# A lasting weight ring of five tiles instead of three, and one weight tile in the memory of the expert sum

## The chip, the core and the metric

The kernel runs on one core of a Trainium2 chip, as one launch. The metric is the time of that launch on the device in microseconds, the median of several runs. The engines of the core work through their own instruction streams and wait for each other by semaphores: TensorE (PE) multiplies matrices, VectorE (DVE), ScalarE (ACT) and GpSimd (POOL) work elementwise, SyncE (SP) does nothing but issue DMA transfers. ScalarE and GpSimd issue some transfers, too.

## The reference

The reference is a network of two layers on 256 tokens x and, beside them, 256 context tokens, all of width 1024. Cut to what matters:

```python
for l in range(2):
    mod = silu(c) @ w_ada[l] + b_ada[l]              # six vectors of 1024; the same for the context
    h = x * (1 + mod[1]) + mod[0]
    parts = split(h @ w_in[l])                       # 1024 -> 2592 columns
    y = concat(diff_attention(parts[0:3]), mla_attention(parts[3:6]), retention(parts[6:10])) @ w_out[l]
    x = layer_norm(ALPHA * x + mod[2] * y)
    h = x * (1 + mod[4]) + mod[3]
    tokens = concat(h, h_of_context)                 # the context in the first layer alone
    scores = sigmoid(tokens @ router_w)              # 16 experts in 4 groups; best group, best 2 in it
    f = sum over the two chosen experts e of gate[e] * (silu(tokens @ w1[e]) * (tokens @ w3[e])) @ w2[e]
    x = layer_norm(ALPHA * x + mod[5] * f)
```

All is float32. The weights are some 300 MB, and each is read once, or in the part that is needed.

## The kernel before, in words

The weights come as tiles of 128 x 2048 float32, 1.05 MB each. The class `Stream` (from line 124) owns them. A list written in advance (`want_ada`, `want_win`, `want_wout`, `want_exp`, up to line 333) sets the order in which they are used, and so the order in which SyncE loads them: the modulation weights `w_ada`, the input projection `w_in`, the output projection `w_out`, then the experts of the layer, and the same for the second layer. Tiles live in rings. A ring (`add_ring`, line 140) is a pool of so many buffers; `pump` (line 154) issues a load for the next tile of the list as long as a ring has a free buffer, and `done` gives a buffer back behind the last instruction that reads the tile. The next load into that buffer waits for that instruction. A newly made ring is filled at once. Besides rings there are rooms (`add_rooms`): memory that belongs to something else and holds one weight tile each until it is wanted.

The lasting ring has RA tiles and exists for the whole program. Per layer there are two more, of sizes RB: one that exists from the end of the attention, and one that is added when the routing is known. The second layer has a ring of four half tiles beside them. The first expert tiles of a layer can be loaded before the routing is known (a tile of the plan stands for one or two experts, and most are fixed in advance); `known` marks how many.

Float32 weights are mostly used in two parts: a rounded high part (`wh`, a cast on ScalarE or, for the first two output-projection tiles, on GpSimd at line 415) and the rest (`wl`, a subtraction on VectorE or GpSimd, line 416 or 1223), with three products for each on TensorE.

The order in which instructions stand on each engine is found by a scheduler, which plays the program through with estimated times, except in stretches where TensorE's order is written out by hand. A changed ring therefore also changes the order elsewhere. Each DMA that SyncE or ScalarE issues takes one of eight semaphores in turn, and can only be issued when the transfer that used it before has landed.

Lines that are spoken of: 187 and 183 (loads of whole tiles and of halves), 1160 (loads of the inputs `xs`), 658 (transposes of `xs`), 530 and 499 (modulation products), 430 to 432 (the three products of a projection), 905, 921 and 942 (transposes in the attention), 558 (transposes of `rt`, the modulation rows), 1644, 1741, 1616 (expert products), 1679 (stores of finished expert rows `yd`), 574 (loads of layer-norm rows), 1962 (gathers `fr` of expert rows), 221 (the helper that records all of ScalarE's and VectorE's work).

Of the kernel before, what the change touches and what calls it, by code (L numbers as in the profile page):

```python
# [23 lines left out]
LAM_INIT = [0.8 - 0.6 * math.exp(-0.3 * l) for l in range(DEPTH)]  # L24
NE = 16
BIG = 8192.0

CHUNKS = [("q", 384), ("k", 384), ("v", 384), ("m", 416), ("qg", 512), ("kv", 512)]
CHUNK_COLS = {
# [196 lines left out]
def build(tc, x_in, ctx_in, wada, win, wout, wexp, wqkv, rw, prm_in, bro_in, lnr, cst_in, out, dbg=None):  # L226
    nc = tc.nc
# [3 lines left out]
    G, T, S = nc.gpsimd, nc.tensor, nc.sync  # L231
# [104 lines left out]
    ws = Stream(nc, aps, widths)  # L336
# [5 lines left out]
    hlp = es.enter_context(tc.tile_pool(name="hlp", bufs=4))  # L342
    ps = es.enter_context(tc.tile_pool(name="ps", bufs=2, space=PS))
    dr = es.enter_context(tc.tile_pool(name="dr", bufs=1, space=DRAM))
    RA, RB = 3, ((4, 3), (3, 6))

    cst = cp.tile([128, NCST], F32, name="cst")
    prm = cp.tile([128, NPRM], F32, name="prm")
# [48 lines left out]
    def level():  # L397
        load["A"] = load["V"] = 0.0
# [10 lines left out]
    def split(raw, n, pool=None, tags=("wh", "wl"), sub=None, high=None, into=None):  # L409

        h, lo = into() if into else ((pool or hlp).tile([128, 1024], F32R, tag=t, name=t) for t in tags)
        if high is None:
            A.copy(h[:, :n], raw)
        else:
            high.tensor_copy(h[:, :n], raw)
        (sub or V).tensor_tensor(lo[:, :n], raw, h[:, :n].bitcast(F32), op=ALU.subtract)
        return h[:, :n], lo[:, :n]
# [717 lines left out]
    x1t = {}  # L1135
# [45 lines left out]
    for l in range(DEPTH):  # L1181
        last = l == DEPTH - 1
# [14 lines left out]
        def wout_half(pool, tags):  # L1197
            for half in range(2):
                raw = ws.take()
                for q in range(2):  # L1200
                    pieces.append(split(raw[:, 1024 * q:1024 * q + 1024], 1024, pool, tags, V if pool else G, high=None if pool else G))
                ws.done()

        wout_half(None, ("wh", "wl"))
        by_time = (0, 1, 2, 6, 7, 3, 4, 5)
        for b in by_time:
# [60 lines left out]
        for i in tiles:  # L1267
# [8 lines left out]
            for n in range(2):  # L1276
                o = acc() if n else sbig()[:, 0:512]
                os_.append(o)
                for k in by_time:
                    h, lo = pieces[4 * n + k // 2]  # L1280
                    c = (k % 2) * 512
# [204 lines left out]
        def tiles_beyond():  # L1486

            nxf = small("nxf", [1])
            V.reduce_sum(nxf, VX.rearrange("p m e -> p (m e)"), axis=AX.X)
            nxi = small("nxi", [1], I32)  # L1490
            V.tensor_copy(nxi, nxf)
            return nc.values_load(nxi[0:1, 0:1], min_val=0, max_val=16 * NM,
                                  skip_runtime_bounds_check_because="at most so many tiles for each expert")
# [82 lines left out]
        def ones_at(t):  # L1576

            Os[t] = []
            for i in tiles:
                O = rp_.tile([128, 128], F32, tag="O", name="O", bufs=2 * NT)  # L1580
                for n, s in enumerate(slots_of(l, t)):
                    pos = (pos0 if s < 2 else posm)[:, i, s:s + 1]
                    if n == 0:
                        V.tensor_scalar(O, C("iota"), pos, None, op0=ALU.is_equal)
                    else:
                        V.scalar_tensor_tensor(O, C("iota"), pos, O, op0=ALU.is_equal, op1=ALU.add)
                Os[t].append(O)
# [67 lines left out]
        def hidden(t):  # L1655
            u = us[t]
            tp = tpb()
            for k in range(4):
                T.transpose(tp[:, 128 * k:128 * k + 128], u[:, 128 * k:128 * k + 128], ident)
            uH = ex.tile([128, 4, 128], F32R, tag="uH", name="uH", bufs=2)  # L1660
            d = uH.rearrange("p k t -> p (k t)")
            if len(plan[t]) == 1:
                uL = ex.tile([128, 4, 128], F32R, tag="uL", name="uL", bufs=2)
                A.copy(d, tp)
                V.tensor_sub(uL.rearrange("p k t -> p (k t)"), tp, d.bitcast(F32))
                us[t] = uH, uL
            else:
                copy(d.bitcast(F32), tp)
                us[t] = uH[:].bitcast(F32)
# [104 lines left out]
        if last:  # L1774

            at_slots()
            f = x1t["f"]
            G.memset(f, 0.0)
            gains1 = ex.tile([16, 128], F32, name="gains1")
            for n in range(2):  # L1780
                nc.scalar.dma_start(gains1[8 * n:8 * n + 8], lnr[n, l].rearrange("(k c) -> k c", c=128))
# [19 lines left out]
            def dispatch(j):  # L1801
                xs_of[j] = ex.tile([128, 8, 128], F32, tag="x", name="x", bufs=2)
                pick(xs_of[j], Os[j])

            def to_tokens(j):

                O = Os.pop(j)
                OTs[j] = rp_.tile([128, W], F32R, tag="OT", name="OT", bufs=3)
                transposed_ones(OTs[j], O)
                gms[j] = rp_.tile([128, 1], F32, tag="gp", name="gp", bufs=2)  # L1810
                gates_at(j, O, acc())(gms[j])
# [17 lines left out]
            with tc.manual_schedule(engines=only_pe):  # L1829
                up(0, [[], [lambda: to_tokens(0)], [], []])  # L1830
                ones_at(1)
                dispatch(1)
                hidden(0)
                down(0)
            level()
            beyond = tiles_beyond()
            m5r = ex.tile([128, 1024], F32, name="m5r")
# [85 lines left out]
        else:  # L1923
# [17 lines left out]
            def rows_of_tokens():  # L1941
                V.tensor_scalar(off_, posm, 127.5, BIG, op0=ALU.is_gt, op1=ALU.mult)
                V.tensor_scalar(place_, posm, 0.0, BIG, op0=ALU.is_lt, op1=ALU.mult)
                V.tensor_tensor(off_, off_, place_, op=ALU.add)
                V.tensor_tensor(place_, posm, C("row0")[:, None, :].to_broadcast([128, NT, 16]), op=ALU.add)
                V.tensor_tensor(place_, place_, off_, op=ALU.add)
                V.tensor_reduce(two[:, :, 0], place_, axis=AX.X, op=ALU.min)
                V.tensor_tensor(off_, place_, two[:, :, 0:1].to_broadcast([128, NT, 16]), op=ALU.is_equal)
                V.scalar_tensor_tensor(place_, off_, BIG, place_, op0=ALU.mult, op1=ALU.add)
                V.tensor_reduce(two[:, :, 1], place_, axis=AX.X, op=ALU.min)  # L1950
                V.tensor_scalar_min(two, two, float(ZROW))
                V.tensor_copy(twoi, two)
# [13 lines left out]
            def gather(x, ll):  # L1966

                gi = rp_.tile([128, 1], I32, tag="gi", name="gi", bufs=4)
                V.tensor_scalar(tmpi, ll[:, 1:2], 0.0, BIG, op0=ALU.is_equal, op1=ALU.mult)
                V.scalar_tensor_tensor(gi, ll[:, 1:2], -1.0, tmpi, op0=ALU.add, op1=ALU.add)  # L1970
# [305 lines left out]
```

## Time and profile before

| | us |
|---|---|
| median of 3 runs (lowest to highest) | 1275.64 (1275.26 to 1279.91) |
| profiled execution | 1273.33 |
| its span | 1271.6 |
| TensorE busy in it | 1142.1 (90%) |
| VectorE, ScalarE, GpSimd busy | 658.9, 472.1, 353.7 |
| mean granted TensorE clock | 0.945 of full |

The profile shows one execution. Its span runs from the first to the last instruction; what lies around it is launch and end. A granted clock of 1.00 means 2.4 GHz, 0.50 means 1.2 GHz. In a timeline each row is a run of equal instructions of one engine: start, length, engine, line, operation, what it writes and reads, how many; in brackets the idle time in front of it, and what ended that.

### The profile page before, as it was taken

The numbers are of one execution on the slowest core, as the hardware profiler recorded it, in microseconds if no ns is written. First come the engines' busy times: TensorE is split into PE (matmuls) and PEld (weight loads), VectorE is DVE, ScalarE is ACT, GpSimd is POOL, SyncE is SP. The second block draws the span as 40 slices with busy tenths as digits, with TensorE's granted clock in tenths as the row PEclk, the third lists the DMA queues.
The fourth block names the chain that finished last, engine by engine and source line by source line (L and its number), as shares of the span: only waits on it lengthen the run. The fifth ranks groups of instructions, "written<-read, shape, count | busy, mean of one in ns | idle before, by whom it ended". The sixth has DMA issues, their size and how long they took to land. (4 is left out here: it accounts for less than half of the span.)

```text
span 1271.6 us, 17886 instructions
## 1 busy us (share of the span) xinstructions
PE 1142.1 (90%) x6443; PEld 747.1 (59%) x6443; DVE 658.9 (52%) x1308; ACT 472.1 (37%) x870; POOL 353.7 (28%) x344
## 2 busy tenths in 40 slices
PE   5999999998996898998992889999998699999994
PEld 3898764566785755545351668976556644444431
DVE  3645366636478966546371768437536712222116
ACT  4423456335235554324241355446343210111102
POOL 0332220231044555335154457221221100101002
PEclk8999999998996898999996979999998799999997
DMA  9443008661546799999985212420764899999981
GB/s 365 160 140 130 1 1 322 262 248 65 208 158 237 248 397 413 409 392 414 414 363 132 76 51 79 153 77 16 283 265 169 317 410 408 409 409 408 409 331 58
DMA packets 72301, 311.77 MB, mean 245 GB/s; under 512 B 8576, under 2 KB 9232, under 8 KB 57872
## 3 DMA queue, kind: packets, MB, share of 16 engines
q1 hardware_dynamic: 63376, 287.73, 58.3%
q10 hardware_dynamic: 5952, 14.45, 3.1%
q0 software_dynamic: 2880, 8.39, 2.4%
q8 instruction: 53, 0.87, 0.3%
q14 instruction: 40, 0.33, 0.1%
HBM read 304.70 MB, written 7.93 MB: 246 GB/s over the span
## 5 line engine op out<-in xcount | busy, mean ns | idle before, releaser
L221 DVE TENSOR_TENSOR wl<-w,wh 128x640 fp32r<-128x640 f32 (+3 forms) x134 | 167.9, 1279 | 48.6 <-ACT wh L221 47.5
L221 ACT CAST wh<-w 128x1024 fp32r<-128x1024 f32 (+2 forms) x136 | 132.5, 1004 | 117.6 <-issue 39.8
L1223 POOL TENSOR_TENSOR wl<-w,wh 128x384 fp32r<-128x384 f32 x96 | 132.9, 1411 | 138.8 <-ACT wh L221 121.3
L1644 PE MATMUL s<-w,x 128*64 128x512 f32 (+1 forms) x640 | 115.8, 596 | 0.0
L221 DVE TENSOR_REDUCE mxv<-s 128x2 f32<-128x1024 f32 (+1 forms) x54 | 56.3, 1044 | 48.0 <-PE s L1098 20.1
L221 ACT ACTIVATE P<-s,mxv 128x512 f32<-128x512 f32 (+1 forms) x108 | 65.9, 618 | 41.1 <-DVE mxv L221 22.3
L1741 PE MATMUL s<-w,uH 128*32 128x512 f32 (+1 forms) x480 | 78.5, 595 | 0.0
L1644 PEld LDWEIGHTS s<-w,x 128*64 128x64 f32 (+1 forms) x640 | 33.6, 126 | 64.9 <-issue 61.2
L221 ACT ACTIVATE u<-s 128x512 f32<-128x512 f32 x20 | 11.9, 596 | 130.7 <-PE s L1644 111.2
L1644 PE MATMUL s<-w,xH 128*32 128x512 f32 (+1 forms) x384 | 56.6, 594 | 0.0
L430 PE MATMUL acc<-wh,hH 128*128 128x384 f32 (+3 forms) x148 | 53.1, 361 | 3.7 <-ACT hH L221 3.7
L431 PE MATMUL s<-wl,hH 128*128 128x384 f32 (+2 forms) x148 | 52.9, 357 | 2.9 <-DVE wl L221 2.9
L221 DVE SCALAR_TENSOR_TENSOR u<-u,gp,s 128x512 f32<-128x512 f32 x20 | 14.9, 744 | 77.6 <-ACT u L221 77.6
L221 DVE TENSOR_TENSOR yL<-s,yH 128x512 fp32r<-128x512 f32 x20 | 13.8, 688 | 76.6 <-ACT yH L221 76.5
L430 PE MATMUL s<-wh,hH 128*128 128x384 f32 (+2 forms) x148 | 53.0, 358 | 0.0
L432 PE MATMUL s<-wh,hL 128*128 128x384 f32 (+2 forms) x148 | 52.8, 357 | 0.0
L431 PE MATMUL acc<-wl,hH 128*128 128x384 f32 (+3 forms) x148 | 52.0, 351 | 0.6 <-DVE wl L221 0.6
L432 PE MATMUL acc<-wh,hL 128*128 128x384 f32 (+3 forms) x148 | 50.5, 351 | 0.0
L1741 PEld LDWEIGHTS s<-w,uH 128*32 128x32 f32 (+1 forms) x480 | 23.2, 122 | 45.0 <-issue 41.7
L1616 PE MATMUL s<-wh,xH 128*128 128x512 f32 x128 | 44.1, 428 | 5.4 <-ACT wh L221 5.4
L1616 PE MATMUL s<-wl,xH 128*128 128x512 f32 x128 | 44.3, 422 | 4.1 <-POOL wl L1223 2.1
L1788 POOL TENSOR_TENSOR xr<-xr,lr 128x1024 f32<-128x1024 f32 x4 | 9.4, 2358 | 135.0 <-ACT lr L221 135.0
(527 smaller groups left out, 2509.5 us busy)
## 6 DMA issues: line engine op xcount, KB each, us to landing
w<-in_wexp_dram SPq DMA_DIRECT2D x288, 512.0 KB, 10.1
w<-in_wexp_dram SPq DMA_DIRECT2D x48, 1024.0 KB, 10.4
w<-in_wada_dram SPq DMA_DIRECT2D x45, 1024.0 KB, 6.2
w<-in_win_dram SPq DMA_DIRECT2D x8, 1024.0 KB, 4.7
w<-in_wout_dram SPq DMA_DIRECT2D x8, 1024.0 KB, 6.7
w<-in_win_dram SPq DMA_DIRECT2D x9, 768.0 KB, 4.1
row<-rowd ACTq DMA_DIRECT2D x9, 512.0 KB, 12.6
yd<-rows ACTq DMA_DIRECT2D x18, 256.0 KB, 8.8
```

The source lines that it names most:

```text
L221: return f(*args, **kw)
L430: T.matmul(o, lhsT=lh, rhs=rh, start=start, stop=False, skip_group_check=True)
L431: T.matmul(o, lhsT=lh, rhs=rl, start=False, stop=False, skip_group_check=True)
L432: T.matmul(o, lhsT=ll, rhs=rh, start=False, stop=stop, skip_group_check=True)
L1223: G.tensor_tensor(lo[:, c:], raw[:, c:], h[:, c:].bitcast(F32), op=ALU.subtract)
L1616: T.matmul(o, lhsT=ll if ps_ == 2 else lh, rhs=rl if ps_ == 1 else rh, start=start and j == 0 and not (same and n), stop=stop and j == 2 a ...
L1644: T.matmul(o[r0:r1, halves[c // 2]], lhsT=x[:, kk, r0:r1], rhs=raw[e][:, halves[q]], start=(kk == 0), stop=(kk == 7), skip_group_check=True)
L1741: T.matmul(o[r0:r1, halves[n]], lhsT=u[:, kk, r0:r1], rhs=raw[e][:, halves[n]], start=(kk == 0), stop=(kk == 3), skip_group_check=True)
L1788: G.tensor_tensor(x1[:, i, :], x1[:, i, :], lr, op=op)
```

## The change

The lasting ring gets five tiles instead of three (RA). The two rings of each layer that come later get one tile less each (RB). In the second layer the memory of the expert sum, `f`, becomes a room for one weight tile behind the attention; so the clearing of `f` moves behind the first expert tile. The scratch in which GpSimd's DMAs keep their descriptors shrinks to 2 KB, which makes the room for the larger ring.

```diff
+SCRATCH = 2048
...
-    RA, RB = 3, ((4, 3), (3, 6))
+    RA, RB = 5, ((4, 2), (3, 5))
...
+        if last:
+
+            ws.add_rooms([x1t["f"].rearrange("p i c -> p (i c)")])
         wout_half(None, ("wh", "wl"))
...
             f = x1t["f"]
-            G.memset(f, 0.0)
             gains1 = ex.tile([16, 128], F32, name="gains1")
...
                 hidden(0)
                 down(0)
+            G.memset(f, 0.0)
             level()
...
-    nc = bacc.Bacc("TRN2", target_bir_lowering=False, num_devices=1)
+    nc = bacc.Bacc("TRN2", target_bir_lowering=False, num_devices=1, dynamic_dma_scratch_size=SCRATCH)
```

SyncE at the start of the program, before (`w_...` are tiles of the lasting ring, `room...` rooms for more of them, `xs` the inputs):

```order
L350 DMA prm<-in_prm_dram 128x192
L352 DMA cst<-in_cst_dram 128x128
L187 DMA w_74<-in_wada_dram 128x2048
L187 DMA w_76<-in_wada_dram 128x2048
L187 DMA w_78<-in_win_dram 128x768
L356 DMA cst<-in_cst_dram 128x1221
L1160 DMA xs<-in_x_in_dram 128x1024 x2
L1160 DMA xs<-in_ctx_in_dram 128x1024 x2
L187 DMA roomzqg<-in_wada_dram 128x2048
```

The same place of the changed kernel, whose lines are numbered one higher here:

```order
L351 DMA prm<-in_prm_dram 128x192
L353 DMA cst<-in_cst_dram 128x128
L188 DMA w_74<-in_wada_dram 128x2048
L188 DMA w_76<-in_wada_dram 128x2048
L188 DMA w_78<-in_win_dram 128x768
L188 DMA w_80<-in_wada_dram 128x2048
L188 DMA w_82<-in_wada_dram 128x2048
L357 DMA cst<-in_cst_dram 128x1221
L1161 DMA xs<-in_x_in_dram 128x1024 x2
L1161 DMA xs<-in_ctx_in_dram 128x1024 x2
L188 DMA roomzqg<-in_win_dram 128x768
```

Two modulation tiles now stand ahead of the constants and of the inputs; a projection tile takes the first room.

TensorE towards the end of the first layer's attention, before: the last modulation tiles before the output projection (`w_2363` is the last of them, `w_2328` the third from the end):

```order
L499 MATMUL acc<-w_2268,sc_92 32x512 x4
L499 MATMUL acc<-w_2299,sc_92 32x512 x4
L1096 MATMUL s<-kT,qrT 128x256
L1098 MATMUL s<-kT,qfT 128x256
L1096 MATMUL s<-kT,qrT 128x256
L1098 MATMUL s<-kT,qfT 128x256
L499 MATMUL acc<-w_2328,sc_92 32x512 x4
L905 MATMUL tp<-cst,sq 128x2 x4
L942 MATMUL tp<-cst,P 128x128 x4
L499 MATMUL acc<-w_2334,sc_92 32x512 x4
L942 MATMUL tp<-cst,P 128x128 x8
L499 MATMUL acc<-w_2363,sc_92 32x512 x4
```

The changed kernel, a stretch further ahead, in which its fifth tile from the end, `w_2105`, is multiplied (`qx` times `ST` behind it is line 1073 of before):

```order
L1062 MATMUL s<-rT 128x128 x8
L500 MATMUL acc<-w_2012,sc_96 32x512 x4
L500 MATMUL acc<-w_2037,sc_96 32x512 x4
L500 MATMUL acc<-w_2056,sc_96 32x512 x4
L500 MATMUL acc<-w_2105,sc_96 32x512 x4
L1074 MATMUL acc<-qx,ST 128x128
L1078 MATMUL acc<-AR,zkv 64x128
```

The first output-projection tile takes the buffer of `w_2328` before, and of `w_2105` now.

GpSimd at that time, before (`w_2369` and `w_2402` are the first two output-projection tiles):

```order
L1033 TENSOR_TENSOR kz<-zkv,zeta 128x256 x2
L1081 TENSOR_TENSOR mix<-mix,rT 128x512 x2
L415 CAST wh<-w_2369 128x1024 x2
L415 CAST wh<-w_2402 128x1024 x2
L416 TENSOR_TENSOR wl<-w_2369,wh 128x1024 x2
L416 TENSOR_TENSOR wl<-w_2402,wh 128x1024 x2
```

And now (`w_2338` and `w_2367`):

```order
L1026 TENSOR_TENSOR qx<-rT,dx 128x512 x4
L1082 TENSOR_TENSOR mix<-mix,rT 128x512
L416 CAST wh<-w_2338 128x1024 x2
L1082 TENSOR_TENSOR mix<-mix,rT 128x512
L416 CAST wh<-w_2367 128x1024 x2
L417 TENSOR_TENSOR wl<-w_2338,wh 128x1024 x2
L417 TENSOR_TENSOR wl<-w_2367,wh 128x1024 x2
```

The first pair of casts has moved ahead of the second multiplication of `mix`; the subtractions still come last. In the second layer GpSimd's order is the same as before here.

## Rows read from the trace of the kernel before

**Rows 1.** By windows: TensorE, its loads, DVE, ACT, POOL busy (count), clock, DMA share, GB/s

```profile
32.00:290.00 258.00, 251.81 (x1512) 181.96 (x1504) 142.07 (x291) 109.50 (x257) 67.64 (x80) 1.00 0.44 159
446.00:657.00 211.00, 196.79 (x1106) 112.39 (x1106) 119.20 (x157) 83.76 (x107) 94.10 (x68) 0.98 1.02 408
1017.00:1256.00 239.00, 232.88 (x1384) 101.72 (x1382) 56.48 (x117) 33.50 (x60) 14.79 (x8) 1.00 0.94 374
```

**Rows 2.** Timeline of SyncE at the start: start us, us, queue, line, out<-in

```profile
1.66 0.90 SPq L187 DMA_DIRECT2D w<-in_wada_dram  x2
2.60 0.43 SPq L187 DMA_DIRECT2D w<-in_win_dram  x1
3.07 0.68 SPq L356 DMA_DIRECT2D cst<-in_cst_dram  x1
5.46 0.80 SPq L1160 DMA_DIRECT2D xs<-in_x_in_dram  x2
```

**Rows 3.** Timeline of TensorE at the start, [idle before <-releaser]

```profile
15.19 0.33 PE L658 MATMUL tp<-cst,xs 128*128 128x128 f32 x1 [0.48 <-DMA xs<-in_x_in_dram]
...
17.84 0.45 PE L658 MATMUL tp<-cst,xs 128*128 128x128 f32 x1 [0.60 <-DMA xs<-in_ctx_in_dram]
19.12 0.69 PE L430 MATMUL acc<-wh,hH 128*128 128x384 f32 x1 [0.84 <-ACT hH L221]
```

**Rows 4.** Timelines of TensorE, GpSimd, SyncE where the output projection's tiles are made ready

```profile
250.21 1.91 PE L499 MATMUL acc<-w,sc 128*32 128x512 f32 x12
...
265.37 1.27 POOL L1081 TENSOR_TENSOR mix<-mix,rT 128x512 f32<-128x512 f32 x1 [7.18 <-ACT sq L221]
...
267.70 1.06 PE L499 MATMUL acc<-w,sc 128*32 128x512 f32 x8
...
268.83 16.45 SPq L187 DMA_DIRECT2D w<-in_wout_dram  x4
...
280.26 9.29 POOL L416 TENSOR_TENSOR wl<-w,wh 128x1024 fp32r<-128x1024 f32 x4
...
949.98 9.27 POOL L416 TENSOR_TENSOR wl<-w,wh 128x1024 fp32r<-128x1024 f32 x4
```

**Rows 5.** Timeline of VectorE: instructions on 128x8 elements

```profile
244.44 0.30 DVE L221 SCALAR_TENSOR_TENSOR rt<-modT,prm 128x8 f32<-128x8 f32 x3
...
283.60 3.75 DVE L221 SCALAR_TENSOR_TENSOR hsc<-modT,prm 128x8 f32<-128x8 f32 x4
...
953.26 3.71 DVE L221 SCALAR_TENSOR_TENSOR rt<-modT,prm 128x8 f32<-128x8 f32 x3
```

**Rows 6.** Timeline of TensorE behind these instructions

```profile
289.88 1.84 PE L905 MATMUL tp<-cst,sq 128*128 128x2 f32 x8 [2.28 <-DVE ms L221]
...
959.77 0.40 PE L558 MATMUL tp<-cst,rt 128*64 128x128 f32 x1 [4.97 <-DVE rt L221]
```

**Rows 7.** By windows, the stretches that follow, columns as in rows 1

```profile
289.88:300.86 10.98, 10.67 (x37) 7.86 (x37) 4.99 (x10) 6.78 (x14) 0.00 (x0) 0.54 0.27 97
959.77:966.00 6.23, 6.12 (x24) 4.06 (x25) 4.57 (x13) 4.22 (x12) 0.00 (x0) 0.54 0.02 5
```

**Rows 8.** Timelines of ScalarE and TensorE where the third tile's rows are stored

```profile
493.31 4.45 ACTq L1679 DMA_DIRECT2D yd<-rows  x2
497.87 1.99 ACT L221 CAST wh<-w 128x1024 fp32r<-128x1024 f32 x2 [7.23 <-DMA w<-in_wexp_dram]
...
498.97 1.22 PE L1616 MATMUL s<-wh,xH 128*128 128x512 f32 x2 [3.27 <-ACT wh L221]
```

**Rows 9.** Timelines of ScalarE and VectorE, layer-norm rows of the second layer

```profile
973.33 0.44 ACTq L574 DMA_DIRECT2D row<-rowd  x1
...
980.38 0.69 DVE L221 TENSOR_TENSOR tn<-s,row 128x512 f32<-128x512 f32 x1 [4.73 <-PE s L432]
```

**Rows 10.** DMA issues: out<-in, queue, operation, count, median us to landing

```profile
fr<-yd,twoi POOLq DMA_INDIRECT x8, 6.2
```

**Rows 11.** Waits of TensorE between the layers: us, times, longest

```profile
PE acc L2022 <- DMA fr<-yd,twoi: 23.5, 3, 15.7
```

## The prediction

> **What bounds the kernel now.** I read the table by stages first. Its columns are the busy engines, the granted clock, the DMA share and the rate. In the first layer's expert stage TensorE is busy 196.79 of 211 us while the DMA engines run at a share of 1.02 and 408 GB/s: two limits almost level. In the second layer's TensorE is busy 232.88 of 239 us at full clock. In the first layer's attention it is 251.81 of 258 us [rows 1]. So what an edit adds while TensorE has no other work in its order is paid in full and is not won back in these long stages; what can be saved is time that TensorE idles now, and time that it runs at a low clock behind an idle spell. Next I listed what TensorE waits for, stage by stage, and looked at the same moments in the timelines of the other engines. Five places matter: the start, where it waits for the inputs xs; two spots at the end of the attentions, where it waits for VectorE; one in the first expert stage, where ScalarE is held at its own DMA issues; the loads of the layer-norm rows in the second layer; and the gathers between the layers. Each has its rows below. The chain of waits of the page covers only the last few us and says nothing on them.
>
> The profiled execution took 1273.33 us: a span of 1271.6 and 1.7 around it. It lies 2.3 us under the median of the three runs, 1275.64. I sum against the profiled time and add 2.3 at the end.
>
> **The start: later.** SyncE now sends the first modulation tiles, a projection tile, the constants and then xs [rows 2]. A ring of five fills as soon as it is made, so two more modulation tiles of 1.05 MB go out ahead of the constants and of xs. TensorE's order there is unchanged: the first two tiles, then the transposes of xs; the two added tiles are used only behind the first projections. The two waits for xs at 15.19 and 17.84 are two transfers of 0.52 MB apart, 1.05 MB in 2.65 us, or 396 GB/s [rows 3]; 2.10 MB at that rate are 5.3 us, and at the 408 GB/s of [rows 1] 5.1. I take 5.2, with bounds of 4.5 (if the queue drains a little now before xs arrive) and 6. No cover exists: from 19.12 on TensorE is busy, and everything behind is ordered relative to it. The tiles that land earlier in exchange are not waited for.
>
> **The end of both attentions: earlier.** While GpSimd forms the low halves of the first two output-projection tiles, four instructions in 9.29 us and 9.27 us [rows 4], VectorE's tiny instructions on 128x8 elements crawl: four take 3.75 us in the first layer and three 3.71 in the second, against three in 0.30 us at another time [rows 5]. Behind them TensorE idles 2.28 us at 289.88 and 4.97 us at 959.77 [rows 6], and afterwards runs at a granted clock of 0.54, so mostly at 1.2 and not 2.4 GHz, for 10.98 and 6.23 us [rows 7]. The Trainium skill, in SBUF — State Buffer, section "SBUF: two separate sides", says that VectorE and GpSimd share one pair of ports under an exclusive lock that the first to start holds for its whole instruction, against VectorE instructions with two SBUF inputs or in a two-port mode; the rows agree, with 2.3 us (9.29 / 4) for each GpSimd instruction. By that rule the wait belongs to the moment, and moving GpSimd's work also moves it onto whatever VectorE then does, which is the first rival below.
>
> The larger ring moves that work. A tile of the ring is filled when an older one is used up: the first output tile now takes the place of the third-last modulation tile (used at 267.70, its load issued at 268.83), and with five tiles that of the fifth-last. In the changed order that one is multiplied next to the work that stands at 250.21 now [rows 4]. It stands fourth in a row of four, of 1.06 us each, so the load goes out near 254.4, some 14 us earlier. GpSimd's order lets the first pair of casts pass the second mix multiply, at 265.37, and puts the second pair behind it [rows 4]. That multiply ends at 266.6; two casts of about 1 us, then 9.3 us of low halves: they end near 278.5 instead of 289.5, ahead of the small instructions at 283.60. In the second layer they must end 6 us earlier than 959.25 to clear those at 953.26; the same rings gave 11 in the first, and I take as much. So both stalls should go. What each is worth: in the first layer the idle 2.28 us and, of the slow stretch, TensorE's 10.67 busy us would take some 5.8 at full clock, but ScalarE is busy 6.78 us in it [rows 7], so at most 3.7 are to be had; bounds 1 and 6, and I take 4, since ScalarE's chain is late next. In the second layer 4.97 idle, and of the slow 6.23 at most 1.6, because VectorE needs 4.57 and is late next; bounds 3 and 6.6, I take 5.5. Together 9.5.
>
> **The first expert stage: a longer hold.** Each DMA that SyncE or ScalarE issues uses one of eight semaphores in turn, and waits until the transfer eight before has landed. At 493.31 ScalarE issues two stores of finished rows, and is held 4.45 us for weight halves that are still in flight; its casts follow at 497.87 and TensorE idles 3.27 us [rows 8]. In the changed order these two stores stand behind weights two tiles further down the stream, of which the additional ring tile makes up one: one more tile, 1.05 MB at 408 GB/s, 2.6 us of hold. Bounds 0 (if the rest arrives early) and 5.1 (if the additional tile gives no lead). A similar pair two tiles later may hold for up to 2 us; 0.7. The lead itself is worth little, since TensorE is busy 93% of this stage [rows 1]. For that and for the first projection tiles of the second layer, five of them loaded ahead, I count a gain of 0.5, between 0 and 2.5.
>
> **The second layer: nothing much.** Its loads of layer-norm rows, the last issued at 973.33, now wait on the same semaphores for three halves of expert weights, and stand behind four casts; that is some 4 us. The first use at 980.38 ended a wait for TensorE, not for the rows [rows 9]; I count 0.5, between 0 and 2. The room in the sum's memory, the five free tiles at routing and the later memset feed a stage in which TensorE is busy 97% of the time [rows 1]: 0. One copy less on ScalarE: 0. The gathers that the smaller scratch serves number eight, with 6.2 us to landing [rows 10]; that it limits them is a rival.
>
> **Sum.** 5.2 + 2.6 + 0.7 + 0.5 - 9.5 - 0.5 = -1.0. Profiled: 1272.3. With the 2.3 to the median: 1274.6.
>
> **The rivals.**
> (a) The port wait moves and is not removed: GpSimd's 9.3 us meet other small VectorE work between 269 and 279 us, or ScalarE's chain ends last anyway, and TensorE gets nothing back. Then 5.2 + 2.6 + 0.7 + 0.5 stand alone: 1284.6, slower. For it: the slow stretches have ScalarE and VectorE nearly as busy as TensorE would be at full clock [rows 7]. Against it: the 128x8 instructions come in one batch, and the first layer's only at 283.60. It decides as soon as the two stalls give back less than 2.6 of their 9.5 us. The page named above speaks for it.
> (b) All of the stalls and of the slow stretches go (12.6 us), the stores are not held longer, and the deeper rings give 1.5: 5.2 - 12.6 - 1.5 = -8.9, 1266.7, faster. For it: both intervals begin at full clock and fall only behind the idle spell. Against it: what is late next has little slack.
> (c) The scratch of 2 KB doesn't hold the descriptors of gathers sent back to back. If each of the eight had to wait for the one before, they would take 8 x 6.2 = 50 us, about twice the 23.5 us that TensorE waits for them now [rows 11]; some 26 us more, 1301. Against it: nothing in the trace shows a gather waiting to be issued.
> (d) The change does not do what it says: the loads at the start pass xs, and the output tiles come no earlier. Then nothing moves, 1275.6.
>
> **How the numbers follow.** A difference under 0.5%, about 6.4 us, can't be told from none: faster is under 1269.3, slower over 1282.0. My forecast, with losses and gains within a few us of each other, 0.53 (its own range 1269 to 1281), (a) 0.15, (b) 0.25, (c) 0.03, (d) 0.04. The bounds of the terms added up give -11 to +11 us; the ends are unlikely together, and 8 in 10 should lie between 1265 and 1284. Faster 0.26: (b) and a little of the forecast's lower end, less (b)'s own misses. Slower 0.18: (a) and (c). The same 0.56.
>
> **What would show it.** The first projection matmul at about 24.3 instead of 19.12. GpSimd's low halves of the output projection ending before the 128x8 instructions begin, these taking 0.3 us and not 3.7, no idle spell before the squares' transposes and the rt transpose, and a granted clock near 1 behind them. ScalarE's pair of row stores held about 7 us, and an idle spell of some 6 us on TensorE behind it. I am wrong if the start moves by less than 3 us, if small VectorE instructions are stretched elsewhere, if the clock stays low without an idle spell, or if the gathers' issues stretch.

## The result: slower by 1.2%, and where the trace after shows it

| | before | after |
|---|---|---|
| median of the four runs timed together, us | 1276.82 | 1293.22 (1287.91; 1293.16 to 1293.28) |
| ratio of the times | | 1.0124 (95%: 1.0101 to 1.0147) |
| profiled execution, its span, us | 1273.33, 1271.6 | 1287.91, 1286.0 |
| TensorE busy, span less busy, us | 1142.1, 129.5 | 1143.7, 142.3 |

The forecast was 1274.6 with a range of 1265 to 1284: the sum had a gain of 1.0 us, and the change costs 16.4, clear of the interval. The profiled execution is the fastest of the four; its span is 14.4 us longer than that of before, which is a fast one of its kernel, too (1273.33 us, against medians of 1276.8 to 1278.0 in this table and in the rounds below). To find the places I took the same matmul in both traces, counted from the start, and wrote down how much later it begins:

| matmul (line of before) | before | after | later by |
|---|---|---|---|
| first projection product, L430 | 19.12 | 24.09 | 4.97 |
| attention of layer 0, scores, L968 | 176.65 | 181.02 | 4.37 |
| its last stretch, L1098 | 276.12 | 286.99 | 10.87 |
| behind the squares' transposes, L950 | 301.92 | 308.69 | 6.77 |
| first expert rows placed, L1992 | 403.02 | 410.09 | 7.07 |
| behind the routing, L1644 | 451.41 | 461.44 | 10.03 |
| last expert tile, L1616 | 661.32 | 676.58 | 15.26 |
| projections of layer 1, L430 | 782.07 | 798.79 | 16.72 |
| modulation rows of layer 1, L509 | 952.27 | 971.67 | 19.40 |
| experts of layer 1, L1644 | 1021.25 | 1035.78 | 14.53 |

The table has the loss and two gains. Start: 5.0 lost, 0.6 of it returned by a higher clock (granted 1.00 from 19 to 40 us, 0.87 from 19 to 36 before). First attention: 6.5 lost before its end and 4.1 gained at its end. Then 0.3 up to the first expert rows, 3.0 at the routing, 5.2 in the first expert stage, 1.5 between the layers, 2.7 in the second attention; 4.9 gained at its end.

How far can such a table be trusted? e2 below has, on all four engines, the order of before through the whole first layer, and its trace still falls 2.5 us behind at the routing and 2.6 in the first expert stage; e1, with the order of before throughout, stays within 0.2 us in both. So at these two places the 3.0 and the 5.2 can't be put down to the change from one trace alone.

The table by stages, for nearly the same work as in [rows 1] (columns as there):

```profile
36.40:299.00 262.60, 255.83 (x1516) 183.19 (x1508) 137.03 (x290) 108.59 (x256) 65.53 (x80) 0.99 0.43 161
456.50:672.20 215.70, 199.12 (x1102) 114.44 (x1102) 120.83 (x158) 81.20 (x105) 89.44 (x66) 0.96 1.01 397
1031.60:1270.60 239.00, 232.81 (x1383) 101.57 (x1382) 56.23 (x115) 33.46 (x60) 16.59 (x9) 1.00 0.94 372
```

The first stretch takes 4.6 us more and almost all of that is TensorE's busy time (255.83 against 251.81), not idle time. The third is as long as before, as the sum had it.

The start, SyncE and TensorE, to be laid beside [rows 2, 3]:

```profile
3.08 2.31 SPq L188 DMA_DIRECT2D w<-in_wada_dram  x2
6.15 0.82 SPq L1161 DMA_DIRECT2D xs<-in_x_in_dram  x2
```

```profile
20.02 0.48 PE L659 MATMUL tp<-cst,xs 128*128 128x128 f32 x1 [5.00 <-DMA xs<-in_x_in_dram]
24.09 0.69 PE L431 MATMUL acc<-wh,hH 128*128 128x384 f32 x1 [0.98 <-ACT hH L222]
```

Two tiles pass xs, and TensorE waits 5.00 us for it where it waited 0.48.

The ends of the attentions, GpSimd, VectorE, TensorE and a window, beside [rows 4 to 7]:

```profile
280.55 9.30 POOL L417 TENSOR_TENSOR wl<-w,wh 128x1024 fp32r<-128x1024 f32 x4
```

```profile
288.49 1.22 DVE L222 TENSOR_REDUCE mxv<-s 128x2 f32<-128x1024 f32 x1 [2.31 <-PE s L1099]
294.68 0.40 DVE L222 SCALAR_TENSOR_TENSOR hsc<-modT,prm 128x8 f32<-128x8 f32 x4
972.66 0.31 DVE L222 SCALAR_TENSOR_TENSOR rt<-modT,prm 128x8 f32<-128x8 f32 x3
```

```profile
974.12 0.30 PE L559 MATMUL tp<-cst,rt 128*64 128x128 f32 x1
```

```profile
300.93:311.90 10.97, 9.49 (x45) 6.39 (x46) 4.28 (x8) 7.79 (x18) 0.00 (x0) 0.84 0.00 0
```

The four small instructions take 0.40 and not 3.75 us, the three 0.31 and not 3.71. TensorE no longer waits for rt, and the clock in the stretch behind the squares is 0.84, not 0.54.

What was not foreseen stands in the modulation products. First the group of these products, by line and shape (busy time, mean ns of one, idle time before them), in the trace before and in the one after; then TensorE's timeline after:

```profile
L499 PE MATMUL acc<-w,sc 128*32 128x512 f32 x320 | 45.7, 602 | 1.1 <-DMA w<-in_wada_dram 1.0
```

```profile
L500 PE MATMUL acc<-w,sc 128*32 128x512 f32 x320 | 50.5, 635 | 0.0
```

```profile
217.62 0.70 PE L969 MATMUL s<-KQ,QR 32*128 32x256 f32 x4 [2.19 <-ACT P L222]
...
233.06 1.05 PE L500 MATMUL acc<-w,sc 128*32 128x512 f32 x4
...
234.67 1.04 PE L500 MATMUL acc<-w,sc 128*32 128x512 f32 x2
...
255.52 1.38 PE L1062 MATMUL s<-rT 64*128 64x128 f32 x16 [2.31 <-DVE AR L222]
256.83 5.21 PE L500 MATMUL acc<-w,sc 128*32 128x512 f32 x32
```

A modulation tile has four products on four quarters of TensorE's columns, and each product leaves two records, so a whole tile is x8. [Rows 4] have a whole tile in 1.06 us. Here half a tile (x4) takes 1.05, and a single product (x2) 1.04 us. The new order cuts ten of the forty tiles of both layers in two, the old one five, and the same 320 records are busy 4.8 us longer. Beside it there are two idle spells of over 2 us that before did not have at these places, and behind both the granted clock falls, where before was granted 1.00 [rows 1]:

```profile
217.00:225.00 8.00, 7.38 (x44) 3.38 (x44) 5.08 (x12) 4.96 (x14) 0.00 (x0) 0.79 0.46 168
255.00:262.00 7.00, 6.48 (x49) 2.22 (x49) 4.01 (x19) 0.00 (x0) 0.00 (x0) 0.76 0.31 96
```

The four whole tiles behind the second spell take 5.21 us for that reason, so a part of the 4.8 us is clock and not cuts.

### The profile page after: what moved, and what is told of

It reads as the page before. It is cut to its first block, busy times and chain, and to the rows that moved or that the text cites. A ratio compares the mean times of both kernels' runs of the same rounds, so it can differ in the third digit from the quotient of the medians.

```text
span 1286.0 us, 17871 instructions
## 1 busy us (share of the span) xinstructions
PE 1143.7 (89%) x6443; PEld 748.0 (58%) x6443; DVE 651.1 (51%) x1308; ACT 472.1 (37%) x869; POOL 354.7 (28%) x344
## 5 line engine op out<-in xcount | busy, mean ns | idle before, releaser
L222 DVE TENSOR_TENSOR wl<-w,wh 128x640 fp32r<-128x640 f32 (+3 forms) x133 | 165.8, 1274 | 49.4 <-ACT wh L222 48.4
L1227 POOL TENSOR_TENSOR wl<-w,wh 128x384 fp32r<-128x384 f32 x96 | 135.7, 1440 | 140.1 <-ACT wh L222 117.1
L500 PE MATMUL acc<-w,sc 128*32 128x512 f32 x320 | 50.5, 635 | 0.0
```

Source lines behind the costliest of these rows:

```text
L222: return f(*args, **kw)
L500: T.matmul(box["o"][32 * c:32 * c + 32, :], lhsT=sc32[:, k, :], rhs=w[:, 512 * c:512 * c + 512], start=(k == 0), stop=(k == 7), skip_group ...
L1227: G.tensor_tensor(lo[:, c:], raw[:, c:], h[:, c:].bitcast(F32), op=ALU.subtract)
```

## The experiments

Each is the kernel named with the edit shown; times are medians, and ratios are to the kernel before in the same rounds.

**e1: the scratch alone.**

```diff
(before) +SCRATCH = 2048
-    nc = bacc.Bacc("TRN2", target_bir_lowering=False, num_devices=1)
+    nc = bacc.Bacc("TRN2", target_bir_lowering=False, num_devices=1, dynamic_dma_scratch_size=SCRATCH)
```

> The kernel before with the DMA scratch of 2 KB and nothing else; every engine's order is that of before. My theory (the loss of the change is the later start plus a new order of the instructions in the attentions and around the routing): no difference, within 0.3% of before, and TensorE waits for the gathers fr 23.5 us in three waits as before. Rival (the small scratch holds GpSimd's gathers back: in the changed kernel the longest of these waits is 18.8 us instead of 15.7): the longest wait grows to 18 us or more, and the time by 2 to 4 us.

1277.29 us, ratio 0.9992 (0.9971 to 1.0012). TensorE's waits for the gathers, in this kernel and in the changed one:

```profile
PE acc L2023 <- DMA fr<-yd,twoi: 23.5, 3, 15.7
```

```profile
PE acc L2026 <- DMA fr<-yd,twoi: 25.3, 3, 18.8
```

With the small scratch alone they are those of [rows 11]. The rival falls. The 1.8 us more in the changed kernel fit GpSimd's order, by its timelines before and after:

```profile
661.34 6.34 POOL L1223 TENSOR_TENSOR wl<-w,wh 128x384 fp32r<-128x384 f32 x4 [11.02 <-ACT wh L221]
667.84 1.01 POOL L1962 DMA_INDIRECT fr<-yd,twoi  x1 [0.16 <-issue]
```

```profile
676.61 9.41 POOL L1227 TENSOR_TENSOR wl<-w,wh 128x384 fp32r<-128x384 f32 x6 [11.02 <-ACT wh L222]
686.16 1.00 POOL L1966 DMA_INDIRECT fr<-yd,twoi  x1
```

Six subtractions instead of four stand ahead of the first gather, 3.07 us. This is read from the rows; no run moved them.

**e2: the room and the later memset alone.**

```diff
(before) +        if last:
+            ws.add_rooms([x1t["f"].rearrange("p i c -> p (i c)")])
...
-            G.memset(f, 0.0)
...
+            G.memset(f, 0.0)
```

> The kernel before with the room in the sum's memory and the later memset, rings and scratch as before; TensorE's order differs only in the second layer's attention end. My theory: the room costs and gives nothing, within 0.3% of before. Rival (one weight tile more in flight at the end of the second attention is what delays the row loads, seen in the changed kernel as a new idle spell of 1.9 us before the LayerNorm transposes): an idle spell of 1 to 2 us appears there and the time grows by 1 to 3 us.

1278.91 us, ratio 1.0005 (0.9984 to 1.0025). An idle spell of 1.17 us does stand in front of these transposes, at 1006.62, as the rival has it (under 0.5 before, 1.90 in the changed kernel). But the time does not grow, so the room is worth nothing, as counted.

**e3: three tiles in the first fill.**

```diff
(changed) -    ws.add_ring(ring, RA, "w", 10 ** 9)
+    ws.add_ring(ring, RA, "w", 10 ** 9, most=3)
```

> The changed kernel, but the ring of five is filled with only three tiles at first; the other two are loaded behind xs. TensorE's order equals the changed kernel's except at the first projections and for a few rows around 310 us; VectorE's order around the routing is nearly that of before. My theory: first projection matmul at 19 to 19.5 instead of 24.1 us; the two idle spells in the first attention (2.2 us before the scores and 2.3 us before s<-rT) stay, as the order there stays; the idle spell of 4.3 us before the products of gts and O shrinks to about the 1.9 us of before. Together 7 us faster than the changed kernel, about 1286 against its 1293. Rival (the idle spells come from transfers that the deeper ring moves, not from the order): the spells in the attention shift or go once the loads at the start stand as before, and the spell before gts and O stays at 4 us.

1276.54 us, ratio 0.9992 (0.9970 to 1.0014): 16.7 less than the changed kernel, far more than I expected. TensorE at the start and at the routing:

```profile
18.89 0.69 PE L431 MATMUL acc<-wh,hH 128*128 128x384 f32 x1 [0.78 <-ACT hH L222]
...
416.82 1.28 PE L1596 MATMUL acc<-gts,O 128*128 128x4 f32 x10 [1.42 <-DVE gts L222]
...
420.47 1.22 PE L1620 MATMUL s<-wh,xL 128*128 128x512 f32 x2 [1.80 <-DVE xL L222]
```

In the changed kernel, VectorE and TensorE at the routing:

```profile
429.76 0.41 DVE L222 TENSOR_TENSOR s<-slot_of,gt 128x256 f32<-128x256 f32 x1
...
432.81 0.40 DVE L222 TENSOR_REDUCE gts<-s 128x16 f32<-128x256 f32 x1
```

```profile
433.27 1.01 PE L1596 MATMUL acc<-gts,O 128*128 128x4 f32 x4 [4.34 <-DVE gts L222]
```

The start is back (5.7 us with the clock), the spells in the attention stay as the theory had it (2.19 at 211.94 and 2.33 at 244.77), and the spell before gts and O goes, as VectorE's order there is that of before. Between its product and its sum the changed kernel puts 2.6 us of other instructions. But e3 loses 3.0 us between the fifth and the sixth place of the table all the same: it waits 1.80 us for xL, as shown, and 1.49 for wl at 437.13. e2 has the same two waits (1.79 and 1.46) and loses 2.5. So the spell goes with VectorE's order, and what that order costs at the routing is not shown. What I had missed: with eight cut tiles instead of ten the first attention loses 5.2 us less, and its end gains some 3 us more. Two cuts of about 0.9 us are not all of that; the order there is a third one, and the rest is open. Against before, e3 is 6.3 us early at 397 us and 1.8 late at 656, so the first expert stage and the routing lose 8 us without a late start, too.

**e4: a ring of three until the first output projection, two tiles more from there.**

```diff
(changed) -    RA, RB = 5, ((4, 2), (3, 5))
+    RA, RB = 3, ((4, 2), (3, 5))
...
+        if not last:
+            ws.add_ring(ring, 2, "v", 10 ** 9)
...
```

> The changed kernel with a ring of three until the first layer's output projection, and two further tiles from there on. TensorE's order in the first attention is that of before; from the second layer's attention on it is that of the changed kernel. My theory: start at 19.1 us as before, no idle spell over 1 us between 180 and 260 us; the 2.3 us spell before the transposes of the squares and its stretch at half clock come back, since the output projection's tiles are loaded as late as before; from the first expert stage on the losses of the changed kernel are as they are there. Time: before plus the 7.5 us that the changed kernel lost between 395 and 661 us, plus 2 at the gathers, minus 3 in the second attention: 1282 to 1285. Rival (the expert stage's losses come from the late start, which shifts the loads against the work): the expert stage then loses nothing, and the time is 1273 to 1276.

1287.02 us, ratio 1.0076 (1.0059 to 1.0094). SyncE's timeline shows that the edit does less than planned, since nothing holds the two free tiles back:

```profile
14.99 0.33 SPq L188 DMA_DIRECT2D w<-in_wout_dram  x1
...
17.56 0.33 SPq L188 DMA_DIRECT2D w<-in_wexp_dram  x1
18.88 0.33 SPq L188 DMA_DIRECT2D w<-in_win_dram  x1
```

They take an output-projection and an expert tile at 15 and 17.6 us, ahead of a projection tile, and cost 3.7 us by 69 us. The stall at the squares comes back, as expected, though smaller: GpSimd waits for the output projection's tiles until 281.27, its low halves run beside the four small instructions, and these crawl.

```profile
290.19 5.15 DVE L222 SCALAR_TENSOR_TENSOR hsc<-modT,prm 128x8 f32<-128x8 f32 x4
```

```profile
295.77 1.02 PE L906 MATMUL tp<-cst,sq 128*128 128x2 f32 x8 [1.58 <-DVE ms L222]
```

The clock behind this spell is 0.85, not the 0.54 of before. From 193 to 254 us (by the times of before) the delay only goes from 3.65 to 4.2, and to 6.6 by 287, where the changed kernel's goes from 4.4 to 10.9: with TensorE's order of before, this stage costs less than half of it. At 657 us the delay is 12.7, so the expert stage loses here as well.

**e5 and e6: the four products together,** in the changed kernel and in the one before.

```diff
-                for c in range(4):
-                    T.matmul(box["o"][32 * c:32 * c + 32, :], ...)
+                first = one(0)
+                with tc.issue_after(first.ins), tc.high_priority():
+                    for c in range(1, 4):
+                        one(c)
```

> The changed kernel, but the four products of a modulation tile (32x512 each, on four quarters of TensorE's columns) always stand next to each other in TensorE's order. In the changed kernel ten of the forty tiles behind the projections are cut in two by other work, in the kernel before five. My theory: four products that stand together take 1.05 us and one or two alone take as much, so each cut costs about 0.9 us of TensorE's busy time; ten cuts less are 5 to 9 us, of which some was time in which TensorE would else have waited: 1286 to 1289 instead of 1293, and the busy time of TensorE falls by 5 us or more. Rival (the cuts are harmless, they fill waits): busy time falls but idle time grows as much, 1292 to 1294.

> The kernel before with the same edit, the four products of a modulation tile together; five cuts less. My theory: 3 to 5 us faster than before, 1272 to 1274. Rival (the cuts fill waits): no difference, 1277.

e5: 1280.99 us, ratio 1.0031 (1.0012 to 1.0050), 12.2 less than the changed kernel; TensorE's busy time falls from 1143.7 to 1133.1. e6: 1277.26, ratio 0.9991 (0.9973 to 1.0009): nothing. The products' group in e5, e6:

```profile
L500 PE MATMUL acc<-w,sc 128*32 128x512 f32 x320 | 41.1, 620 | 4.1 <-DMA w<-in_wada_dram 2.1 <-DVE U L222 2.0
```

```profile
L499 PE MATMUL acc<-w,sc 128*32 128x512 f32 x320 | 42.2, 616 | 6.2 <-DMA w<-in_wada_dram 6.2
```

The group's busy time is 9.4 us less without the ten cuts (50.5 less 41.1); some 1.6 of that is the clock behind the second spell, since four tiles that stand together take 5.21 us there and 3.64 in e5. Busy and idle together are 46.8 before, 50.5 after, 45.2 in e5, 48.4 in e6. So both theories hold, each for one kernel: before, the cuts fill waits for tiles in flight; with a ring of five more tiles lie ready, and over half of what the cuts cost is loss. e5 still has two idle spells in the first attention (2.19 and 1.96 us).

**e7: row stores on GpSimd.**

```diff
(changed) -                    nc.scalar.dma_start(yd[...], rows)
+                    G.dma_start(yd[...], rows)
```

> The changed kernel with the stores of finished expert rows yd issued by GpSimd instead of ScalarE; the order of TensorE is that of the changed kernel but for four rows. GpSimd's transfers have semaphores of their own, so that no store waits for weight halves in flight. My theory: ScalarE isn't held at these stores; the idle spells of TensorE before the products at 511 us (3.6 us) and 556 us (4.0 us) shrink to 1.5 us or less, and the time falls by 4 to 6 us, to 1287 to 1289. Rival (ScalarE's casts wait for the weights themselves, the hold only stands in front of that wait): both spells stay within 1 us of what they are, and the time is 1292 to 1294.

1284.57 us, ratio 1.0044 (1.0023 to 1.0065), 8.7 less. In the changed kernel, ScalarE and TensorE, beside [rows 8]:

```profile
506.94 3.21 ACTq L1683 DMA_DIRECT2D yd<-rows  x2
...
552.27 2.90 ACTq L1683 DMA_DIRECT2D yd<-rows  x2
```

```profile
511.70 0.74 PE L1620 MATMUL s<-wh,xH 128*128 128x512 f32 x2 [3.55 <-ACT wh L222]
...
556.39 0.74 PE L1620 MATMUL s<-wh,xH 128*128 128x512 f32 x2 [4.02 <-ACT wh L222]
```

In e7 both spells are gone. Ahead of the first place e7 falls 4.0 us behind the changed kernel, since TensorE waits 3.06 us for VectorE at 489 us and its granted clock there is 0.66:

```profile
486.00:496.00 10.00, 6.94 (x18) 5.33 (x18) 7.88 (x7) 3.14 (x3) 5.87 (x6) 0.66 1.02 422
```

So the first place gives little: at 508 us (by the times of before) e7 is 1.7 us ahead of the changed kernel. Behind the second place, at 555, it is 5.2.

**e8: all three edits in the changed kernel** (those of e3, e5 and e7).

> The changed kernel with three edits: three tiles in the first fill, the four products together, the row stores on GpSimd. My theory: the edits act at different places and add up, 1276.5 less 5 less 5, 1264 to 1269, and faster than both kernels. Rival (they share the same slack, the DMA engines bound the first expert stage): 1274 to 1277, as with the smaller first fill alone.

1262.19 us, ratio 0.9888 (0.9856 to 0.9919): 15.8 us less than before and faster than both kernels. Alone the edits gave 16.7, 12.2 and 8.7 us, 37.6 in all; together they give 31.0. So most of it adds up, and some is shared. Its modulation products are as short as in e5, with less waiting:

```profile
L500 PE MATMUL acc<-w,sc 128*32 128x512 f32 x320 | 41.0, 620 | 1.6 <-DMA w<-in_wada_dram 1.4
```

And the first expert stage gains instead of losing: against before, e8 is 5.9 us early behind the routing and 10.9 at the last expert tile. One stretch of time, before, in the changed kernel and in e8 (the work in it is not quite the same, since the kernels are up to 16 us apart there):

```profile
440.00:560.00 120.00, 112.70 (x713) 68.74 (x715) 74.49 (x110) 52.55 (x69) 57.74 (x43) 0.97 1.00 399
```

```profile
440.00:560.00 120.00, 109.78 (x677) 69.54 (x676) 76.22 (x105) 57.74 (x73) 59.56 (x46) 0.97 0.96 373
```

```profile
440.00:560.00 120.00, 115.28 (x743) 66.98 (x743) 73.08 (x110) 51.53 (x67) 62.65 (x54) 0.99 1.01 404
```

In the changed kernel the DMA engines move 373 GB/s and TensorE is busy 109.78 us; in e8 it is 404 and 115.28.

**e9: the changed kernel again.**

> The changed kernel once more, beside the kernel before in the same rounds: its first four times were 1287.9 and three of 1293.2, so that the size of the loss is uncertain by some 5 us. My theory: its times spread as those of the other kernels do, median 1287 to 1293, and the profile repeats the places of the loss: first projection at 24 us, ten modulation tiles cut in two, 4 us before the products of gts and O, 3 to 4 us at the second of the held row stores. Rival (a further loss of some 5 us that the first trace doesn't show): a new place with 3 us or more, or a stretch at half clock that the first trace lacks.

1291.92 us, ratio 1.0115 (1.0087 to 1.0144). All places return. The span is 1290.8 us, 4.8 longer than in the first trace, and TensorE is busy 1149.3 us, 5.6 more, with the same instructions in the same order. One stretch with the same work, in the first trace and in e9:

```profile
642.82:650.87 8.05, 5.29 (x26) 3.54 (x25) 7.30 (x8) 7.12 (x9) 5.20 (x4) 1.00 1.02 414
```

```profile
644.23:654.31 10.08, 7.69 (x26) 5.57 (x24) 9.34 (x9) 7.26 (x9) 7.21 (x5) 0.66 1.01 410
```

TensorE waits 1.73 us for ScalarE in both, and behind that wait the granted clock stays at 1.00 in the first and is 0.66 over the stretch in e9, which takes 2.0 us longer. Ahead of another place, at 307 us, the spells differ (1.23 and 2.32 us), and the clock does, too (1.00 and 0.72 over the same work). So the 4.8 us between two executions of one kernel are clock in the main. The 1.8 us between the loss of the profiled executions, 14.6, and that of the medians, 16.4, lie within that.

**e10: the low halves on VectorE, in the kernel before.**

```diff
-  pieces.append(split(raw[...], 1024, pool, tags, V if pool else G, high=None if pool else G))
+  pieces.append(split(raw[...], 1024, pool, tags, V, high=None if pool else G))
```

> The kernel before, in which VectorE and not GpSimd forms the low halves of the first two output-projection tiles of each layer. VectorE gets four instructions of about 1.2 us each more per layer. My theory (VectorE's instructions on 128x8 elements crawl because GpSimd subtracts at the same time): without GpSimd's 9.3 us they take 0.1 us each, the idle spells of 2.3 us at 290 us and 5.0 us at 960 us shrink below 1 us each unless VectorE's own new work stands in front, and the time falls by 3 to 9 us, 1268 to 1274. Rival (they crawl for another reason, such as waits on TensorE's transposes): they still take 0.9 us or more each and the spells stay; 1277.

1271.57 us, ratio 0.9947 (0.9926 to 0.9968). VectorE:

```profile
283.71 0.40 DVE L221 SCALAR_TENSOR_TENSOR hsc<-modT,prm 128x8 f32<-128x8 f32 x4
...
952.82 0.31 DVE L221 SCALAR_TENSOR_TENSOR rt<-modT,prm 128x8 f32<-128x8 f32 x3
```

At the same time as in [rows 5], without GpSimd beside them, they take a ninth of the time or less, and both spells are gone. The rival falls. In this trace the 4.4 us that TensorE is ahead at 391 us are given back in the first expert stage (0.0 at 654), as part of e3's are.

**e11: a ring of four,** the other rings as before.

```diff
(changed) -    RA, RB = 5, ((4, 2), (3, 5))
+    RA, RB = 4, ((4, 3), (3, 6))
```

> The changed kernel with a lasting ring of four, and the other rings as before. One tile ahead of xs instead of two; five modulation tiles cut in two, as before; GpSimd's order at the output projection is that of before, only the tiles come earlier. My theory, by the terms as now measured: start 2.6 us later, no loss from cuts, half of the gain at the ends of the attentions (4 to 5 us), 2 to 5 us lost around the routing, the held stores and the gathers: 1276 to 1282 against 1277 to 1278 of before. Rival (the loss of the changed kernel grows with the ring alone, half of it for half the tiles): 1284 to 1286.

1271.65 us, ratio 0.9971 (0.9952 to 0.9991): less than I expected, and far from the rival's 1284 to 1286. TensorE at the start, and its modulation products with five cuts:

```profile
17.88 0.47 PE L659 MATMUL tp<-cst,xs 128*128 128x128 f32 x1 [2.50 <-DMA xs<-in_x_in_dram]
```

```profile
L500 PE MATMUL acc<-w,sc 128*32 128x512 f32 x320 | 45.1, 601 | 0.7 <-DMA w<-in_wada_dram 0.7
```

TensorE waits 2.50 us for xs and the first projection begins 2.8 us later than before, somewhat more than half of what two tiles cost. The gain at the ends is full, not half (the small instructions take 0.40 us at 284.12), and no cut is added. So the loss does not grow in step with the ring; that it goes with the order that each ring happens to get fits this, but the smaller rings differ here, too.

**e12: the two edits without the ring** (before, products together, row stores on GpSimd).

> The kernel before with the two edits that helped the changed kernel and have nothing to do with its ring: the four products together, and the row stores on GpSimd. It shows what the larger ring is worth once its start is mended (1262.2 us with all three). My theory: the edits give 1 us for the products (as measured alone) and 3 to 4 us for the held pair of stores, 1273 to 1275; the larger ring then is worth 10 us or more, most of it at the ends of the attentions. Rival (the stores and products carry the gain, the ring nothing): 1262 to 1266.

1279.82 us, ratio 1.0018 (1.0000 to 1.0036). I expected 3 us of gain, and there is none. The whole change with its start mended (the larger ring with the small scratch, the room and the order that the scheduler made for them) is then worth some 17 us: 1279.82 less 1262.19 is 17.6, from different rounds, and the two ratios differ by 1.3%.

## Why the prediction was wrong, point by point

- **Start, +5.2.** Right: 4.97, and it goes with e3. One tile costs 2.8 in e11.
- **Ends of the attentions, -9.5.** Right: -4.1 and -4.9, with the signs named (small instructions short, no spell, higher clock). e10 shows the cause. Rival (a), that the wait moves to other work of VectorE, did not come: during GpSimd's 9.30 us a TENSOR_REDUCE that reads PSUM took its usual 1.22 us.
- **First attention ahead of its end, counted as 0.** This is the step that failed most: "TensorE's order there is unchanged" was said of the start, and of the attention I looked only at where the fifth-last tile stands. The scheduler gave TensorE a new order over 80 us, which cuts six tiles instead of three and leaves two new spells, with a lower clock behind them: 6.5 us. e5, which keeps the four products together, gets 7 us back there; e4, with the order of before, loses 2.9.
- **Second attention ahead of its end, counted as 0.** 2.7 us; four cuts there instead of two. e5 returns 0.9 of it; the rest is open.
- **Routing, counted as 0.** 3.0 us. The spell in front of the products of gts and O goes with VectorE's order (1.4 us in e3; 3.9 in e5, e7 and e9, with the order of the changed kernel; 1.9 in e1 and e2). That the 3.0 us come from it is not shown: e3 loses as much there without that spell, and e2 2.5 with the order of before.
- **Held stores, +2.6 and +0.7.** The sum is short, and the places are reversed: the first pair, counted as the larger loss, is held 3.21 us, less than the 4.45 of before; the second is held 2.90, and TensorE's spell there is 4.02. The whole stage costs 5.2; behind the second pair e7 is 5.2 ahead of the changed kernel. What else moves in this stage, where the DMA engines and TensorE are level, gains are given back, and e2 loses 2.6 us with the order of before, is not settled. The step "one more tile, 2.6 us of hold" took the transfers ahead of the store from the order and left out that the work too comes later.
- **DMA lead, -0.5.** +1.5 us between the layers, which fits the two subtractions more ahead of GpSimd's gathers. Rival (c) on the scratch fell in e1.
- **Row loads, +0.5.** Not held, 0:

```profile
992.16 0.81 ACTq L575 DMA_DIRECT2D row<-rowd  x2
993.02 0.46 ACTq L575 DMA_DIRECT2D row<-rowd  x1
```

```profile
997.74 0.69 DVE L222 TENSOR_TENSOR tn<-s,row 128x512 f32<-128x512 f32 x1
```

With the measured terms the sum is 4.4 + 6.5 - 4.1 + 0.3 + 3.0 + 5.2 + 1.5 + 2.7 - 4.9 = 14.6, against a span longer by 14.4. The start and the ends of the attentions were near; 6.5, 2.7 and 3.0 us stood at places that the sum had at nothing, though the order of the changed kernel could be read. Of these, the runs show the first to be TensorE's new order (e5, e4); the other two are open, since no run has five tiles from the start with the order of before on every engine. A slip in the working changes nothing of this: the slow stretch of 10.98 us, with ScalarE busy for 6.78, leaves at most 4.2 and not 3.7. The chances had the same hole: no rival was a worse order.

## What to carry to other kernels

Where a scheduler sets the order, a change of buffers is also a change of order: lay the two orders side by side over every stretch that differs, count what is now cut apart or put in front of a waited-for result, and give it a term and a rival. A buffer that fills earlier than its data is wanted costs its transfer time to whatever stands behind it in the queue, so fill only what is wanted first (e3). Before judging a change by its total, mend its side effects one by one: here they hid some 17 us.

## What the runs showed of the hardware that I had not expected

- Four products of 32 columns on four quarters of TensorE take 1.06 us together, and one alone 1.04. The Trainium skill, in TensorEngine Tiling (Array Packing), section "Key Properties", says that different tiles of the array can run matmuls in parallel; the trace agrees. Other work put between them cost about 0.9 us for each cut here (9.4 us for ten, some of it clock).
- VectorE's instructions whose only input is in PSUM were not stretched beside GpSimd's subtractions: the TENSOR_REDUCE at 288.49 takes what an equal one at 225.38 takes away from them:

```profile
225.38 1.22 DVE L222 TENSOR_REDUCE mxv<-s 128x2 f32<-128x1024 f32 x1 [1.05 <-PE s L969]
```

  The Trainium skill, in SBUF — State Buffer, section "SBUF: two separate sides", names only instructions with two SBUF inputs or in a two-port mode; the trace agrees.
- The same kernel, with the same order, was granted a lower clock in e9 than in its first trace (0.66 against 1.00 behind the same wait of 1.73 us) and took 4.8 us longer; that is a third of the effect under study, so one profile does not size a change of 1%.
